# exp(bias) of six heads in PSUM, and the bias of the next unit put in PSUM early, in a streaming log-sum-exp kernel

## The chip, the cores and the metric

The kernel runs on one core of a Trainium2 chip. The metric is the device time of one execution in microseconds (us). A run's profile also gives a span, from the first to the last instruction, which is some 1.8 us shorter.

## The reference, cut to what matters

```python
B, S, D, H = 8, 2048, 2048, 8          # x: B x S x D fp32 (134 MB), bias: H x 256
x_heads = x.reshape(B, S, H, 256).transpose(0, 2, 1, 3) + bias[None, :, None, :]
x_tiled = np.repeat(x_heads, 2, axis=2)
lse = log-sum-exp of x_tiled over its last axis       # B x H x 2S
```

For each row and head, 256 numbers are summed after an exponential. The kernel doesn't subtract the maximum. It has two ways to bring in the bias: add it before the exponential, or multiply by exp(bias) after it.

## The kernel before

x comes in 64 tiles of 128 partitions x 2 rows x 2048 columns (2 MB) into nine SBUF buffers. The work of each tile is shared by heads:

- **Heads of `pe`** (0 and 1, or 0 alone in tiles 50 to 60): TensorE puts the bias in PSUM with a matmul of ones, adds x with a matmul by the identity, and ScalarE takes exp and the sum in one instruction.
- **Heads from `g0`**: GpSimd adds the bias in place, ScalarE takes exp, VectorE sums.
- **The heads between**: ScalarE takes exp of x alone, and VectorE multiplies by exp(bias) and sums.

The last three tiles (61 to 63) go row by row with no GpSimd addition: heads 2 to 7 are all weighed on VectorE by `weigh`, one instruction per row and head, except that GpSimd *folds* head 7 of tile 62's second row and heads 6 and 7 of tile 63's first row: it multiplies them by exp(bias) and halves them by additions to 32 columns, which VectorE reduces.

```python
W0, G0, W1 = Dh, 4 * Dh, 5 * Dh
w_sb = sb.tile([P, D - W1], F32, name="w_sb")        # exp(bias), heads 5 to 7, SBUF
w_ps = pp.tile([P, W1 - W0], F32, name="w_ps")       # exp(bias), heads 1 to 4, 2 PSUM banks
ps = [pp.tile([P, MM], F32, name=f"ps{i}") for i in range(5)]   # biased rows, 5 banks
tpair = pp.tile([P, 2, K, P], F32, name="tpair")     # transpositions, 1 bank
# ... (cut)
def add_bias(m, t, k0, k1):                          # a unit: a tile, or a row of it
    for ka, kb in groups:
        nc.tensor.matmul(p[:, ...], lhsT=ones3, rhs=each_row(b3, ...), start=True, stop=False)
    for (ka, kb), views in zip(groups, got):
        mm = nc.tensor.matmul(..., lhsT=ident, rhs=xt[:, ka:kb, 0:n], start=False, stop=True)
# ... (cut)
def weigh(t, v, h, dst, after):
    w = w_ps[...] if c < W1 else w_sb[...]
    nc.vector.tensor_tensor_reduce(out=v, in0=v, in1=w, op0=ALU.mult, op1=ALU.add, accum_out=dst, ...)
def fold(t, k, h0, h1, sums, after):
    nc.gpsimd.tensor_tensor(out=v, in0=v, in1=w_sb[...], op=ALU.mult)
    # ... halving additions on GpSimd, then a short tensor_reduce on VectorE (cut)
```

Of the kernel before, what the change touches and what calls it, by code (L numbers as in the profile page):

```python
# [9 lines left out]
F32 = mybir.dt.float32  # L10
# [6 lines left out]
NBUF = 9  # L17
# [29 lines left out]
def kernel(  # L47
# [7 lines left out]
    P = nc.NUM_PARTITIONS  # L55
    B, S, D = x.shape
    H, Dh = bias.shape
    assert D == H * Dh and S % (P * K) == 0
    NBLK = S // (P * K)
    T = B * NBLK  # L60
    CPE = 2 * Dh
    MM = 512

    W0, G0, W1 = Dh, 4 * Dh, 5 * Dh

    sb = ctx.enter_context(tc.tile_pool(name="sb", bufs=1))
    pp = ctx.enter_context(
        tc.tile_pool(name="pp", bufs=1, space=bass.MemoryType.PSUM)
    )
# [3 lines left out]
    w_sb = sb.tile([P, D - W1], F32, name="w_sb")  # L73
# [9 lines left out]
    res = sb.tile([H * NBLK, B - 1, P, K, 2], F32, name="res")  # L83
    res_last = sb.tile([P, P, 2], F32, name="res_last")
    xts = [sb.tile([P, K, D], F32, name=f"xt{i}") for i in range(NBUF)]
    w_ps = pp.tile([P, W1 - W0], F32, name="w_ps")
    ps = [pp.tile([P, MM], F32, name=f"ps{i}") for i in range(5)]
    tpair = pp.tile([P, 2, K, P], F32, name="tpair")
    tps = [tpair[:, i] for i in range(2)]

    def modes_of(t):
        return [modes for t0, modes in STAGES if t0 <= t][-1]

    def pieces(t):

        if len(modes_of(t)) == 1:
            return [(0, K, 0, D)]
        cols = [[(0, D)]] * K if t < T - 1 else LAST_COLS
        return [(k, k + 1, c0, c1) for k in range(K) for c0, c1 in cols[k]]
# [13 lines left out]
    def on_x(t, ins, after):  # L113
        known = [u for u in users[t] if u.ins.engine != ins.ins.engine]
        for before in range(t % NBUF, t, NBUF):
            known += users[before]
        for u in known:
            if u not in after:
                tc.declare_no_dep(
                    ins.ins, u.ins, reason="waited for by those it waits for"  # L120
                )
        users[t].append(ins)
        return ins
# [21 lines left out]
    for set_idx, (_name, funcs) in enumerate(get_activation_tables(nc.m.arch).items()):  # L145
        if ACT.Exp in funcs and ACT.Ln in funcs:
            nc.scalar.add_instruction(
                mybir.InstLoadActFuncSet(
                    name=nc.get_next_instruction_name(),
# [22 lines left out]
    def spread(dst, c0, c1):  # L172
        nc.tensor.matmul(  # L173
            dst, lhsT=ones, rhs=brow[:, c0:c1], start=True, stop=True
        )

    for i, c in enumerate(range(G0, D, MM)):
# [1 line left out]
        nc.scalar.activation(  # L179
            out=b_rep[:, c - G0 : c - G0 + MM], in_=ps[i], func=ACT.Copy  # L180
        )
    for c in range(W0, W1, MM):
        w = w_ps[:, c - W0 : c - W0 + MM]
        spread(w, c, c + MM)
        nc.scalar.activation(out=w, in_=w, func=ACT.Exp)  # L185
# [2 lines left out]

    n_ps = [0]

    def add_bias(m, t, k0, k1):


        n = m["pe"] * Dh
        xt = xts[t % NBUF]
        step = MM // n
        groups = [(k, min(k + step, k1)) for k in range(k0, k1, step)]
        got = []
        for ka, kb in groups:
            p = ps[n_ps[0] % len(ps)]  # L200
            n_ps[0] += 1
            nc.tensor.matmul(  # L202
                p[:, 0 : (kb - ka) * n],
                lhsT=ones3,
                rhs=each_row(b3, 0, n, kb - ka),
                start=True,
                stop=False,
            )
            got.append([p[:, k * n : (k + 1) * n] for k in range(kb - ka)])
        rows = []  # L210
        for (ka, kb), views in zip(groups, got):
            p = views[0]
            mm = nc.tensor.matmul(  # L213
                bass.AP(
                    tensor=p.tensor,
                    offset=p.offset,
                    ap=[p.ap[0], [1, (kb - ka) * n]],
                ),
                lhsT=ident,
                rhs=xt[:, ka:kb, 0:n],  # L220
                start=False,
                stop=True,
            )
            on_x(t, mm, [loads[t, k0, 0]])
            rows += [(v, mm) for v in views]
        return rows

    def sum_biased(m, t, k, p, mm, sums):
# [11 lines left out]
    def each_row(src, c, n, k_rows):  # L240

        return bass.AP(
            tensor=src.tensor,
            offset=src.offset + c,
            ap=[src.ap[0], [0, k_rows], [1, n]],
        )

    def g_add(m, t, k0, k1):
        c = m["g0"] * Dh
        v = xts[t % NBUF][:, k0:k1, c:D]  # L250
        add = nc.gpsimd.tensor_tensor(  # L251
            out=v, in0=v, in1=each_row(b_rep, c - G0, D - c, k1 - k0), op=ALU.add
        )
        return on_x(t, add, [loads[t, k0, 0]])

    def exp_inplace(t, v, after):
        return on_x(t, nc.scalar.activation(out=v, in_=v, func=ACT.Exp), [after])  # L257
# [23 lines left out]

    def weigh(t, v, h, dst, after):
        c = h * Dh
        w = w_ps[:, c - W0 : c - W0 + Dh] if c < W1 else w_sb[:, c - W1 : c - W1 + Dh]
        ttr = nc.vector.tensor_tensor_reduce(  # L285
            out=v,
            in0=v,
            in1=w,
            scale=1.0,
            scalar=0.0,  # L290
            op0=ALU.mult,
            op1=ALU.add,
            accum_out=dst,
        )
        last_uses[t].append(on_x(t, ttr, [after]))

    def fold(t, k, h0, h1, sums, after):


        v = xts[t % NBUF][:, k, h0 * Dh : h1 * Dh]  # L300
        done = nc.gpsimd.tensor_tensor(  # L301
            out=v, in0=v, in1=w_sb[:, h0 * Dh - W1 : h1 * Dh - W1], op=ALU.mult
        )
        on_x(t, done, [after])
        v = v.rearrange("p (h j) -> p h j", j=Dh)
        n = Dh
        while n > FOLD:
            n //= 2
            done = nc.gpsimd.tensor_tensor(  # L309
                out=v[:, :, 0:n], in0=v[:, :, 0:n], in1=v[:, :, n : 2 * n], op=ALU.add  # L310
            )
            on_x(t, done, [])

        def add_up():
            red = nc.vector.tensor_reduce(
                out=sums[:, k, h0:h1],
                in_=v[:, :, 0:FOLD],
                op=ALU.add,
                axis=mybir.AxisListType.X,
            )  # L320
            on_x(t, red, [done])

        return add_up
# [40 lines left out]
    def sums_of(t):  # L364

        b, blk = divmod(t, NBLK)
        if b < B - 1:
            return R[b][:, :, :, blk]
        return R_last[:, :, blk, :].rearrange("p h k -> p k h")
# [3 lines left out]
    for_pool = []  # L373
    for_pe = []

    def flush(later_work):
        for f in later_work:
            f()
        later_work.clear()

    for t in range(T):
        xt = xts[t % NBUF]
        sums = sums_of(t)
        for k0, k1, c0, c1 in pieces(t):
            m = modes_of(t)[k0]
            add = None
            if c0 == 0:
                got = add_bias(m, t, k0, k1)
                if m["g0"] < H:
                    add = g_add(m, t, k0, k1)  # L390
            if c0 == 0 and (t < T - 1 or k0 == 0):
                flush(for_pool)
            h0 = max(c0 // Dh, m["pe"])
            h1 = min(c1 // Dh, m["g0"])
            hf = max(h0, min(h1, H - m["fold"]))
            if h0 < h1 and not m["late"]:
                done = exp_inplace(
                    t, xt[:, k0:k1, h0 * Dh : h1 * Dh], loads[t, k0, c0]
                )
                if hf < h1:  # L400
                    for_pool.append(fold(t, k0, hf, h1, sums, done))
            if c0 == 0 and (t < T - 1 or k0 == 0):
                flush(for_pe)
            if not m["late"]:
                for k in range(k0, k1):
                    for h in range(h0, hf):
                        weigh(
                            t,
                            xt[:, k, h * Dh : (h + 1) * Dh],
                            h,  # L410
                            sums[:, k, h : h + 1],
                            done,
                        )

            def pool_part(t=t, m=m, k0=k0, k1=k1, sums=sums, add=add):
                if add:
                    later(m, t, k0, k1, sums, add)
                if k1 == K and t + NBUF < T:
                    load(t + NBUF)

            def pe_part(t=t, m=m, got=got, k0=k0, k1=k1, sums=sums):
                for k in range(k0, k1):
                    sum_biased(m, t, k, *got[k - k0], sums)

            for_pool.append(pool_part)
            if c0 == 0:
                if m["g0"] < H:
                    pe_part()
                else:
                    for_pe.append(pe_part)  # L430

        fb, at = divmod(t - 2, NBLK)
        if fb >= 0 and at == NBLK - 1:
            finish(fb)
            if fb == B - 2:
                store()
    flush(for_pe)
    flush(for_pool)
    finish_last()
# [32 lines left out]
```

## Time and profile before

| | before |
|---|---|
| time, median of the first 3 runs | 329.07 us (328.91 to 329.17) |
| span of the profiled run (its time: 328.65 us) | 326.8 us |
| x read | 134.23 MB, at 427 GB/s from 92 to 295 us |
| busy: VectorE, ScalarE, GpSimd, TensorE | 88%, 85%, 88%, 71% |
| last VectorE sum ends, transposition starts | 323.2, 323.45 us |

Read it from the last row up. The DMA engines are busy until nearly the end, and what remains after the last x has landed is a chain through the engines. Only work on that chain can move the end.

### The profile page before, as it was taken

The page shows a single profiled execution, that of the slowest core. Times are in us where ns is not written, and L with a number is a line of the kernel's source. Part 1 is how long each engine was busy: PE and PEld are TensorE (multiplying, and loading weights), DVE is VectorE, ACT ScalarE, POOL GpSimd, SP SyncE. Part 2 cuts the span into 40 slices and gives each one's busy share as a digit, 9 for nine tenths or more (in the row PEclk, how much of TensorE's full clock was granted, in tenths as well). Part 3 has the DMA queues.
Part 4 walks back from the last instruction along what each step waited for, and adds up shares of the span by engine and source line. Part 5 has one row for each costly group of instructions (what it writes and reads, how often), then busy time and mean ns, then how long its engine had stood idle before and what let it go on. Part 6 is the DMA issues. An engine that isn't in the chain of part 4 may idle for free.

```text
span 326.8 us, 1954 instructions
## 1 busy us (share of the span) xinstructions
PE 231.0 (71%) x389; PEld 67.6 (21%) x389; DVE 287.5 (88%) x318; ACT 277.7 (85%) x573; POOL 288.6 (88%) x88
## 2 busy tenths in 40 slices
PE   5499666667897689667658767767678756665784
PEld 2023211112221212211212212212212101222210
DVE  0019999999999999999998999999998999999995
ACT  3269999699889888989889889899888988799994
POOL 6999899979999999999999999999998999999623
PEclk9999898598568955887698778778965555555577
DMA  8999999999999999999999999999999999999993
GB/s 294 432 429 435 422 429 429 427 425 435 419 435 428 421 437 424 425 433 425 426 434 419 424 437 421 431 431 423 433 428 421 439 423 420 421 420 419 421 384 91
DMA packets 11807, 135.41 MB, mean 414 GB/s; under 512 B 1361, under 2 KB 1489, under 8 KB 2833
## 3 DMA queue, kind: packets, MB, share of 16 engines
q1 hardware_dynamic: 11696, 135.27, 98.3%
q8 instruction: 3, 0.05, 0.1%
q14 instruction: 10, 0.08, 0.1%
q10 hardware_dynamic: 2, 0.01, 0.0%
q0 software_dynamic: 96, 0.00, 0.0%
HBM read 134.23 MB, written 1.05 MB: 414 GB/s over the span
## 4 chain that ended last, share of the span: by engine, by line
DMA 58%; DVE 21%; ACT 8%; POOL 8%; PE 4%; issue 1%; SPq 0%; DVEq 0%
DMA xt<-in_x_dram 55%; DVE R L274 14%; ACT xt L257 7%; POOL xt L251 6%; DVE xt L267 5%; PE ps L213 3%; DMA b<-bparts 2%; DVE xt L285 1%; ACT xt L232 1%; DMA brow<-in_bias_dram 1%; PE ps L202 1%; POOL xt L309 0%; POOL brest L164 0%; POOL brest L166 0%; POOL xt L301 0%
## 5 line engine op out<-in xcount | busy, mean ns | idle before, releaser
L251 POOL TENSOR_TENSOR xt<-xt,b_rep 128x2048 f32<-128x2048 f32 (+1 forms) x66 | 277.4, 4212 | 21.1 <-DMA xt<-in_x_dram 21.0
L213 PE MATMUL ps<-xt,ident 128*128 128x512 f32 (+1 forms) x244 | 177.8, 861 | 75.0 <-DMA xt<-in_x_dram 74.8
L257 ACT ACTIVATE xt<-xt 128x3072 f32<-128x3072 f32 (+3 forms) x91 | 185.6, 2063 | 18.6 <-POOL xt L251 18.2
L274 DVE TENSOR_REDUCE R<-xt 128x12 f32<-128x3072 f32 (+1 forms) x56 | 181.4, 3240 | 2.0 <-ACT xt L257 0.3
L232 ACT ACTIVATE xt<-ps 128x256 f32<-128x256 f32 x234 | 87.0, 396 | 15.9 <-PE ps L213 15.7
L267 DVE TENSOR_TENSOR xt<-xt,w_ps 128x1024 f32<-128x1024 f32 x50 | 60.9, 1218 | 32.8 <-ACT xt L257 32.7
L213 PEld LDWEIGHTS ps<-xt,ident 128*128 128x128 f32 x244 | 55.5, 257 | 153.5 <-DMA xt<-in_x_dram 111.6
L202 PE MATMUL ps<-b,ones 3*128 3x512 bf16 (+1 forms) x122 | 48.3, 463 | 6.1 <-DMA b<-bparts 3.7
L232 ACT ACTIVATION_READ_ACCUMULATOR xt<-ps 128x1 f32 x234 | 51.6, 222 | 0.0
L285 DVE CUSTOM_DVE_ANT_0 xt<-xt,w_ps 128x256 f32<-128x256 f32 x84 | 30.2, 416 | 0.0
L202 PEld LDWEIGHTS <-ones 3*128 3x128 bf16 x122 | 7.9, 97 | 79.7 <-issue 79.7
L274 DVE TENSOR_REDUCE R_last<-xt 128x4 f32<-128x1024 f32 x10 | 12.2, 1217 | 0.0
L301 POOL TENSOR_TENSOR xt<-xt,w_sb 128x256 f32<-128x256 f32 (+1 forms) x2 | 2.1, 1057 | 8.5 <-ACT xt L257 8.5
L330 PE MATMUL tpair<-ident,R 128*64 128x128 f32 x14 | 3.5, 340 | 5.8 <-DVE R L274 5.8
L285 DVE CUSTOM_DVE_ANT_0 xt<-xt,w_sb 128x256 f32<-128x256 f32 x15 | 6.8, 495 | 0.0
L173 PE MATMUL ps<-brow,ones 1*128 1x512 f32 x4 | 3.7, 1089 | 3.4 <-DMA brow<-in_bias_dram 3.4
L340 ACT ACTIVATE res<-tpair 64x512 f32<-64x512 f32 x7 | 4.1, 582 | 2.2 <-PE tpair L330 2.2
L285 DVE DVE_READ_ACCUMULATOR2_ANT R_last<- 128x1 f32 x63 | 5.2, 82 | 0.0
L179 ACT ACTIVATE b_rep<-ps 128x512 f32<-128x512 f32 x2 | 1.2, 597 | 4.6 <-PE ps L173 4.6
L173 PE MATMUL w_ps<-brow,ones 1*128 1x512 f32 x4 | 4.0, 1096 | 0.7 <-ACT w_ps L185 0.7
L330 PEld LDWEIGHTS tpair<-ident,R 128*64 128x64 f32 x14 | 1.7, 140 | 12.0 <-DVE R L274 9.7
L185 ACT ACTIVATE w_ps<-w_ps 128x512 f32<-128x512 f32 x2 | 1.2, 582 | 3.3 <-PE w_ps L173 3.3
(24 smaller groups left out, 18.3 us busy)
## 6 DMA issues: line engine op xcount, KB each, us to landing
xt<-in_x_dram SPq DMA_DIRECT2D x56, 2048.0 KB, 31.9
xt<-in_x_dram SPq DMA_DIRECT2D x14, 1024.0 KB, 21.0
xt<-in_x_dram SPq DMA_DIRECT2D x5, 256.0 KB, 11.3
out_dram<-res SPq DMA_DIRECT2D x1, 896.0 KB, 7.9
xt<-in_x_dram SPq DMA_DIRECT2D x2, 384.0 KB, 16.5
out_dram<-res_last SPq DMA_DIRECT2D x1, 128.0 KB, 1.7
b<-bparts POOLq DMA_DIRECT2D x3, 1.0 KB, 5.6
brow<-in_bias_dram ACTq DMA_DIRECT2D x1, 8.0 KB
```

What stands on the lines that cost most here:

```text
L173: nc.tensor.matmul(dst, lhsT=ones, rhs=brow[:, c0:c1], start=True, stop=True)
L202: nc.tensor.matmul(p[:, 0 : (kb - ka) * n], lhsT=ones3, rhs=each_row(b3, 0, n, kb - ka), start=True, stop=False,)
L213: mm = nc.tensor.matmul(bass.AP(tensor=p.tensor, offset=p.offset, ap=[p.ap[0], [1, (kb - ka) * n]],), lhsT=ident, rhs=xt[:, ka:kb, 0:n], s ...
L232: act = nc.scalar.activation(out=xts[t % NBUF][:, k, c : c + Dh], in_=p[:, c : c + Dh], func=ACT.Exp, accum_out=sums[:, k, h : h + 1],)
L251: add = nc.gpsimd.tensor_tensor(out=v, in0=v, in1=each_row(b_rep, c - G0, D - c, k1 - k0), op=ALU.add)
L257: return on_x(t, nc.scalar.activation(out=v, in_=v, func=ACT.Exp), [after])
L267: mul = nc.vector.tensor_tensor(out=f, in0=f, in1=each_row(w_ps, h0 * Dh - W0, n, k1 - k0), op=ALU.mult,)
L274: red = nc.vector.tensor_reduce(out=sums[:, k0:k1, h0:H], in_=v.rearrange("p k (h j) -> p k h j", j=Dh), op=ALU.add, axis=mybir.AxisListTy ...
L285: ttr = nc.vector.tensor_tensor_reduce(out=v, in0=v, in1=w, scale=1.0, scalar=0.0, op0=ALU.mult, op1=ALU.add, accum_out=dst,)
L301: done = nc.gpsimd.tensor_tensor(out=v, in0=v, in1=w_sb[:, h0 * Dh - W1 : h1 * Dh - W1], op=ALU.mult)
L330: nc.tensor.transpose(out=tp[0:nr, k], in_=R[b][:, k].rearrange("p h n -> p (h n)"), identity=ident,)
L340: nc.scalar.activation(out=res[:, b], in_=tv, func=ACT.Ln)
```

## The change

The intent is twofold. Heads 5 and 6 join those whose exp(bias) lies in PSUM; w_ps grows from two banks to three, and the biased rows lose a bank. And TensorE is to have the bias of the next unit in PSUM already when its x lands.

```diff
-    W0, G0, W1 = Dh, 4 * Dh, 5 * Dh
+    W0, G0, W1, W2 = Dh, 4 * Dh, 6 * Dh, 7 * Dh
...
-    w_ps = pp.tile([P, W1 - W0], F32, name="w_ps")
-    ps = [pp.tile([P, MM], F32, name=f"ps{i}") for i in range(5)]
+    w_ps = pp.tile([P, W2 - W0], F32, name="w_ps")
+    ps = [pp.tile([P, MM], F32, name=f"ps{i}") for i in range(4)]
...
-    for c in range(W0, W1, MM):
+    for c in range(W0, W2, MM):
...
-    def add_bias(m, t, k0, k1):
+    def put_bias(m, k0, k1):        # the bias matmuls of a unit
...
+    def add_x(m, t, k0, got):       # its x matmuls
...
-        w = w_ps[...] if c < W1 else w_sb[...]
+        w = w_ps[...] if c < W2 else w_sb[...]
...
+    bias_there = put_bias(*next_units.pop(0))
...
-                got = add_bias(m, t, k0, k1)
+                got = add_x(m, t, k0, bias_there)
+                if next_units:
+                    bias_there = put_bias(*next_units.pop(0))
```

More of the change, by code (lines that the diff above doesn't have):

```diff
@@ L189 @@
     n_ps = [0]
-    def add_bias(m, t, k0, k1):
+    def put_bias(m, k0, k1):
         n = m["pe"] * Dh
-        xt = xts[t % NBUF]
         step = MM // n
-        groups = [(k, min(k + step, k1)) for k in range(k0, k1, step)]
         got = []
-        for ka, kb in groups:
-            p = ps[n_ps[0] % len(ps)]
+        for ka in range(k0, k1, step):
+            kb = min(ka + step, k1)
+            p = ps[n_ps[0] % len(ps)][:, 0 : (kb - ka) * n]
             n_ps[0] += 1
             nc.tensor.matmul(
-                p[:, 0 : (kb - ka) * n],
+                p,
                 lhsT=ones3,
@@ L208, in add_bias @@
             )
-            got.append([p[:, k * n : (k + 1) * n] for k in range(kb - ka)])
+            got.append((ka, kb, p))
+        return got
+    def add_x(m, t, k0, got):
+        n = m["pe"] * Dh
         rows = []
-        for (ka, kb), views in zip(groups, got):
-            p = views[0]
+        for ka, kb, p in got:
             mm = nc.tensor.matmul(
-                bass.AP(
-                    tensor=p.tensor,
-                    offset=p.offset,
-                    ap=[p.ap[0], [1, (kb - ka) * n]],
-                ),
+                p,
                 lhsT=ident,
-                rhs=xt[:, ka:kb, 0:n],
+                rhs=xts[t % NBUF][:, ka:kb, 0:n],
                 start=False,
@@ L224, in add_bias @@
             on_x(t, mm, [loads[t, k0, 0]])
-            rows += [(v, mm) for v in views]
+            rows += [(p[:, k * n : (k + 1) * n], mm) for k in range(kb - ka)]
         return rows
@@ L283, in weigh @@
         c = h * Dh
-        w = w_ps[:, c - W0 : c - W0 + Dh] if c < W1 else w_sb[:, c - W1 : c - W1 + Dh]
+        w = w_ps[:, c - W0 : c - W0 + Dh] if c < W2 else w_sb[:, c - W1 : c - W1 + Dh]
         ttr = nc.vector.tensor_tensor_reduce(
@@ L374 @@
     for_pe = []
+    next_units = [
+        (modes_of(t)[k0], k0, k1)
+        for t in range(T)
+        for k0, k1, c0, _ in pieces(t)
+        if c0 == 0
+    ]
+    bias_there = put_bias(*next_units.pop(0))
     def flush(later_work):
```

## The prediction

> **What bounds the kernel now.** I read the time of every engine first, then the slices of the span, then the chain that ended last, and then the tail instruction by instruction, because each of these views sends the reader on to the next. From the profile page of the kernel before, the slices:
>
> ```profile
> DVE  0019999999999999999998999999998999999995
> ACT  3269999699889888989889889899888988799994
> POOL 6999899979999999999999999999998999999623
> DMA  8999999999999999999999999999999999999993
> q1 hardware_dynamic: 11696, 135.27, 98.3%
> HBM read 134.23 MB, written 1.05 MB: 414 GB/s over the span
> ```
>
> The DMA row is at nine tenths from the second slice to the last but one, and the queue of the x loads takes 98.3% of what the 16 engines have. Table of stretches: 427 GB/s from 92 to 295 us and 423 from 295 to 310. At 427 GB/s the 134.23 MB take 314 us of a span of 326.8. So the body of the kernel is a stream of x; VectorE (88%), ScalarE (85%) and GpSimd (88%) follow just behind. Something that shortens only their work or TensorE's in the body cannot bring the end forward. The remaining 12 us or so lie after the last data, and there an engine's work counts. The chain of waits of the last 12 us (start us, duration us, what):
>
> ```profile
> 294.92 19.81 DMA xt<-in_x_dram
> ...
> 314.75 1.49 ACT xt L257
> ...
> 316.31 0.86 POOL xt L301
> ...
> 318.58 0.19 DVE R_last L315
> 318.76 1.31 DVE xt L285
> ...
> 320.09 0.33 DVE xt L285
> ...
> 322.83 0.34 DVE xt L285
> ...
> 323.45 0.32 PE tpair L351
> ```
>
> The end is set by VectorE: after the reduction at 318.58, eleven weighted sums (exp(x) times exp(bias), summed over a head, L285) run without a gap; ten of them step by 0.34 us, the first takes 1.31 us of the chain. Then come a short reduction, one transposition, one logarithm and the store, 326.8 - 323.45 = 3.35 us that the change does not touch. The timeline shows who that first one is and what is beside it (start us, duration us, engine, line, operation):
>
> ```profile
> 317.90 0.53 DVE L285 CUSTOM_DVE_ANT_0 xt<-xt,w_sb 128x256 f32<-128x256 f32 x1
> 318.53 1.27 POOL L301 TENSOR_TENSOR xt<-xt,w_sb 128x512 f32<-128x512 f32 x1
> 318.68 1.40 DVE L285 CUSTOM_DVE_ANT_0 xt<-xt,w_sb 128x256 f32<-128x256 f32 x1
> 320.01 0.41 DVE L285 CUSTOM_DVE_ANT_0 xt<-xt,w_ps 128x256 f32<-128x256 f32 x1
> ```
>
> The slow one takes its weight from SBUF (w_sb), starts 0.15 us after a GpSimd multiply of two SBUF operands, and ends at 320.08, 0.28 us after GpSimd does (319.80). Its neighbour with the weight in PSUM takes 0.41 us. By tile: 15 instructions with w_sb take 414/422/1398 ns (shortest/median/longest), 84 with w_ps 408/416/422. PSUM itself is no faster; it only escapes what GpSimd does.
>
> **What the Trainium skill says.** "SBUF — State Buffer", section "Who interferes with whom": VectorE and GpSimd share a pair of ports under an exclusive lock; a VectorE instruction with two SBUF inputs contends with a GpSimd one that reads SBUF, whichever comes first blocks the other for a whole instruction, and a VectorE instruction with at most one SBUF input, outside the two-port modes, does not contend. The trace agrees: 1.40 us against 0.42, and never over 0.422 us in 84 cases with w_ps. "PSUM — Partial Sum Buffer", "Specifications (TRN2)": 8 banks of 512 fp32 values per partition. So w_ps goes from 2 banks to 3, the biased rows (ps) from 5 to 4, and the transpositions keep 1: PSUM is full in both. The same page, "Engine vs sequencer instructions": matmuls start and complete in program order. That decides what the second half of the change can do; the trace's TensorE rows indeed alternate in program order.
>
> **The change, part by part.**
>
> *Bias of the next unit early.* In the program text the bias matmuls move from just ahead of their x matmuls to just behind the x matmuls of the unit before. I compared TensorE's two instruction streams: both are bias 0, x 0, bias 1, x 1, and so on. Nothing lay between x of one unit and the bias of the next except the transpositions of a finished batch, 14 in all at 340 ns (3.5 us); those now stand behind the bias. And before the change the bias already ran ahead of its data: the waits table has TensorE waiting 74.8 us for x in 58 cases, with the bias 3.7 us for its first load and 2.3 us for ScalarE, and nothing else. At 140.66 us the two bias matmuls run, 0.60 us, and the x matmuls follow at 141.94 when their data land. Only 7 pairs of transpositions change place, at most 7 x 0.6 us, all where TensorE waits for x afterwards. Worth to the end: 0.
>
> *Four banks instead of five.* In the body a unit takes two banks. With five, the second bias matmul waits for the first half of the sums of two units back; with four, for the second half, two ScalarE instructions or about 0.36 x 2 = 0.7 us later. The trace shows such waits twice, at 33.13 us (0.76) and 37.24 us (1.51), while ScalarE catches up with the nine tiles loaded at the start. They may become three or four, each up to 0.7 us longer. At that time VectorE has 4 to 5 tiles of backlog and waits for nothing until 91 us, and the loads are queued 31.9 us from issue to landing. In the tail a unit takes one bank: the last bias (319.32) needs the bank of four units back, whose sums ended at 314.4. Worth: 0.
>
> *A third piece of w_ps.* One more fp32 matmul (1.06 us) and one more exp (0.58 us), and 0.25 us less exp for w_sb. Before, the second exp ended at 12.25 us and TensorE then waited until 15.36 us for the bias rows. The third piece: matmul 12.3 to 14.4, exp to 15.0, w_sb until 15.6. ScalarE's first sum is at 18.40. It fits by about 1 us. Worth: 0.
>
> *Heads 5 and 6 weighed from PSUM.* Of the 15 instructions with w_sb only the four of head 7 remain w_sb. (The unit with head 7 folded on GpSimd and the last tile's first row use none on VectorE.) Eight of the eleven that move run at 0.42 either way: nothing. The two at 317.52 (0.46) and 317.90 (0.53) save 0.04 and 0.11, but the reduction at 318.58 that follows waits for GpSimd's fold, which ended at 318.55: hidden. The one at 318.68 goes from 1.40 to 0.41 us and is on the chain: 1.31 - 0.34 = 0.97 us off VectorE.
>
> How much of 0.97 us reaches the end? VectorE then runs behind ScalarE's five exponentials (317.61 to 320.74; 842 ns for the two of 768 columns, 622 for three of 512, overlapping by about 0.1). The second one ends at 317.61 + 0.73 + 0.84 = 319.2, and VectorE would be ready at 319.02: it loses 0.2. Nine sums are then left at 0.34 (three of the first row, six of the second, whose exponentials end at 319.7, 320.2 and 320.74, each in time): 319.25 + 9 x 0.34 = 322.3, plus the reduction 0.21 = 322.5, against 323.3 before. VectorE saves 0.8. But the transposition also needs ScalarE's last sum of the biased heads, which ends at 322.65, released by TensorE's last x matmul (319.85 to 321.78). So the transposition starts at about 322.65 + 0.14 = 322.8 instead of 323.45. The sum is 0.65 us.
>
> **Rivals.**
>
> *A. Full gain of 1 us.* This needs ScalarE's last sum to come earlier as well. TensorE's chain in the tail is load at 314.75, x 2.0, bias 0.5, x 2.0, bias 0.5, x 1.9, at a granted clock of 0.66. If a higher clock is granted there, it shortens by some tenths. The change doesn't cause that. Time: 328.0.
>
> *B. The wait on ScalarE takes the place of the removed one altogether*, or the fold does: GpSimd's last instruction ends at 319.88 + 1.73 = 321.61, and the last reduction waits for it. That is 0.7 us before VectorE gets there, and GpSimd's multiply, no longer met by a VectorE instruction on SBUF, can only end earlier. So the fold is no bound; but if the tail's matmuls get a clock nearer 0.5, the gain shrinks to 0.2 or so. Time: 328.9.
>
> *C. Four banks stall TensorE and through it the sums, the release of buffers and the loads.* This would need TensorE to fall so far behind that a load is issued late; the DMA row would show a dip. Against it: 16 us between the first release (28 us) and the time the stream of nine tiles (4.85 us each) would run dry at 44, and TensorE's idle 75 us. A case of 1 to 3 us is conceivable: 330 to 332. I give it 3%.
>
> *D. TensorE's lead brings the x matmuls forward.* It would show as less waiting of ScalarE for TensorE (15.7 us now). Since the order is the same, I expect none.
>
> **Range and chances.** The median of before is 329.07 us, three runs within 0.26. 329.07 - 0.65 = 328.4. The stream of 134 MB adds its own scatter between builds: 0.1% of its rate is 0.3 us. With A and B at the edges, the range is 327.7 to 329.2. Two per cent would be 6.6 us, more than half of all that lies after the stream, so faster by over 2% has 1%, slower 2%, and within 2% 97%.
>
> **What would show it.** Right: the VectorE weighted sum beside GpSimd's multiply of 512 columns takes 0.41 to 0.42 us; no w_ps instruction exceeds 0.43; the chain before the last transposition passes through ScalarE's sum (L232) or is level with VectorE's; the transposition starts about 0.6 us earlier relative to the last load's landing; DMA stays at 420 GB/s and more. Wrong: a DMA slice below nine tenths in the body, waits of TensorE's bias matmul for ScalarE over some 10 us in sum, a w_ps instruction as slow as 1 us, or a time that moves by over 2 us. The weakest term is the stream itself: a change of its rate by 0.3% would hide all of the gain.

## The result, and the profile after

In the first comparison the changed kernel took 328.07 us (median of 6 runs, 328.03 to 328.42) against 329.0 (6 runs, 328.9 to 329.18): ratio 0.9973, 95% interval 0.996 to 0.9986. Two later sets, below, gave 0.9988 and 0.999, with intervals that reach just above 1: at most some 0.3% faster, never slower by the medians, and in the later sets not told apart from no change.

The slices of the span from the page of the changed kernel, with the load queue:

```profile
DVE  0029999999999999989998999989998999999994
ACT  3279999798889888799889889899888988799995
POOL 7999899979999999999998999999998999999713
DMA  8999999999999999999999999999999999999993
q1 hardware_dynamic: 11696, 135.27, 98.5%
```

The DMA row is the same digit by digit, and the rate from 92 to 295 us is 427 GB/s as before. The body hasn't moved; the span is 326.5 instead of 326.8. The chain that ended last in the changed kernel, its last pieces (start us, duration us, what):

```profile
309.90 10.19 DMA xt<-in_x_dram
...
320.12 0.63 ACT xt L257
...
321.38 1.47 ACT xt L232 x8
322.85 0.04 issue
322.89 0.49 PE tpair L351
```

VectorE is gone from these pieces. The chain is now: x lands, ScalarE's last two exponentials, its four sums of the biased heads, transposition. And the timeline at the place of the slow sum:

```profile
318.53 0.19 DVE L315 TENSOR_REDUCE R_last<-xt 128x1 f32<-128x32 f32 x1 [0.17 <-POOL xt L309]
318.63 1.27 POOL L301 TENSOR_TENSOR xt<-xt,w_sb 128x512 f32<-128x512 f32 x1
318.64 0.41 DVE L285 CUSTOM_DVE_ANT_0 xt<-xt,w_ps 128x256 f32<-128x256 f32 x1
...
319.32 0.42 DVE L285 CUSTOM_DVE_ANT_0 xt<-xt,w_ps 128x256 f32<-128x256 f32 x1 [0.26 <-ACT xt L257]
...
320.12 1.27 ACT L257 ACTIVATE xt<-xt 128x512 f32<-128x512 f32 x2 [0.31 <-DMA xt<-in_x_dram]
```

GpSimd's multiply and VectorE's sum start within 0.01 us of each other and neither is lengthened: 1.27 and 0.41 us. In the kernel before the sum took 1.40. By tile, the shortest, median and longest of all weighted sums of the changed kernel, first those with weights in SBUF, then in PSUM:

```profile
L285 DVE CUSTOM_DVE_ANT_0 xt<-xt,w_sb x4: 420/422/422, 312.1 to 322.1; 128x256 f32<-128x256 f32 x4
L285 DVE CUSTOM_DVE_ANT_0 xt<-xt,w_ps x95: 410/418/422, 262.7 to 321.7; 128x256 f32<-128x256 f32 x95
```

No sum is slow any more.

### The profile page after: what moved, and what is told of

It is laid out like the page before. It is cut to its first block, busy times and chain, and to the rows that moved or that the text cites. A ratio compares the mean times of both kernels' runs of the same rounds, so it can differ in the third digit from the quotient of the medians.

```text
span 326.5 us, 1959 instructions
## 1 busy us (share of the span) xinstructions
PE 230.7 (71%) x391; PEld 67.5 (21%) x391; DVE 286.4 (88%) x318; ACT 278.5 (85%) x574; POOL 288.4 (88%) x88
## 4 chain that ended last, share of the span: by engine, by line
DMA 69%; DVE 10%; POOL 7%; ACT 7%; PE 6%; issue 0%; SPq 0%
DMA xt<-in_x_dram 67%; DVE R L274 7%; POOL xt L251 6%; ACT xt L257 5%; PE ps L217 4%; DVE xt L267 2%; DMA b<-bparts 2%; ACT xt L232 2%; PE ps L202 1%; DMA brow<-in_bias_dram 0%; POOL brest L165 0%; POOL brest L167 0%; POOL b L170 0%; PE tpair L330 0%; POOL bparts L164 0%
## 5 line engine op out<-in xcount | busy, mean ns | idle before, releaser
L217 PE MATMUL ps<-xt,ident 128*128 128x512 f32 (+1 forms) x244 | 175.7, 852 | 78.8 <-DMA xt<-in_x_dram 78.5
L232 ACT ACTIVATE xt<-ps 128x256 f32<-128x256 f32 x234 | 86.8, 394 | 11.2 <-PE ps L217 11.1
L202 PE MATMUL ps<-b,ones 3*128 3x512 bf16 (+1 forms) x122 | 47.5, 457 | 2.8 <-ACT xt L232 1.6
L285 DVE CUSTOM_DVE_ANT_0 xt<-xt,w_ps 128x256 f32<-128x256 f32 x95 | 34.0, 417 | 0.3 <-ACT xt L257 0.3
L174 PE MATMUL w_ps<-brow,ones 1*128 1x512 f32 x6 | 6.0, 1109 | 1.3 <-ACT w_ps L186 1.3
L285 DVE DVE_READ_ACCUMULATOR2_ANT R<- 128x1 f32 x36 | 3.0, 85 | 0.0
```

Of the source, the lines that this page charges most:

```text
L174: nc.tensor.matmul(dst, lhsT=ones, rhs=brow[:, c0:c1], start=True, stop=True)
L202: nc.tensor.matmul(p, lhsT=ones3, rhs=each_row(b3, 0, n, kb - ka), start=True, stop=False,)
L217: mm = nc.tensor.matmul(p, lhsT=ident, rhs=xts[t % NBUF][:, ka:kb, 0:n], start=False, stop=True,)
L232: act = nc.scalar.activation(out=xts[t % NBUF][:, k, c : c + Dh], in_=p[:, c : c + Dh], func=ACT.Exp, accum_out=sums[:, k, h : h + 1],)
L285: ttr = nc.vector.tensor_tensor_reduce(out=v, in0=v, in1=w, scale=1.0, scalar=0.0, op0=ALU.mult, op1=ALU.add, accum_out=dst,)
```

## The experiments

The theory to test: one VectorE instruction (head 5 of the last tile's first row) used to wait for GpSimd, and this is the whole gain. The rivals: the early bias gives it; the bank less costs something; the other ten moved sums matter. Twelve runs were made, in three sets of four: ten new kernels, and the changed kernel twice more; all gave right results. The edits are shortened, and some are shown against the changed kernel ("after, but").

**First set: the parts of the change one by one.** The kernel before took 328.89 us here (9 runs, 328.77 to 329.38).

*weights_only*: three banks of weights and four of biased rows, the bias matmuls where they were.

```diff
 (after, but)
-                got = add_x(m, t, k0, bias_there); bias_there = put_bias(...)
+                got = add_bias(m, t, k0, k1)
```

> Six heads of exp(bias) in PSUM and four banks for the biased rows, but the bias matmuls where they were before the change. Theory (one weighted sum of VectorE in the tail no longer waits for GpSimd): the whole gain of the change is here, 0.6 to 1.0 us less than the kernel before, and the sum beside GpSimd's 512-column multiply takes 0.42 us. Rival (the bias put in PSUM early gives the gain): no gain, within 0.2 us of before.

Measured: 328.25 us (328.11 to 328.86), ratio 0.9982 (0.9969 to 0.9994), and no w_ps sum over 0.422 us. The gain is here, as expected. (In its only trace VectorE started 0.04 us before GpSimd; that matters below.)

*order_only*: the early bias with four heads of weights and five banks.

```diff
 (after, but)
-    W0, G0, W1, W2 = Dh, 4 * Dh, 6 * Dh, 7 * Dh
+    W0, G0, W1, W2 = Dh, 4 * Dh, 5 * Dh, 5 * Dh
-    ... for i in range(4)]
+    ... for i in range(5)]
```

> The bias of the next unit early, but four heads in PSUM and five banks as before the change. Theory: within 0.2 us of the kernel before, because TensorE's order is the same but for 14 transpositions; the slow sum still takes about 1.4 us. Rival (bias early gives the gain): 0.6 to 1.0 us faster.

Measured: 328.76 us (328.25 to 329.1), ratio 0.9993 (0.998 to 1.0005), so the same within what the runs resolve. From its timeline:

```profile
318.65 1.27 POOL L301 TENSOR_TENSOR xt<-xt,w_sb 128x512 f32<-128x512 f32 x1
318.73 1.47 DVE L285 CUSTOM_DVE_ANT_0 xt<-xt,w_sb 128x256 f32<-128x256 f32 x1
```

The slow sum is still there, as expected. But the runs spread over 0.85 us, and one was as fast as the changed kernel.

*banks_only*: the kernel before with `range(4)` for `range(5)` banks, nothing else.

> The kernel before with four banks for the biased rows instead of five, nothing else. Theory: within 0.2 us of before; TensorE's bias matmuls wait for ScalarE somewhat more often (2 to 4 times, 2 to 4 us in sum), all in the first 45 us. Rival (a bank less costs time which the change had to win back): 0.3 us or more slower.

Measured: 328.74 us (328.27 to 329.16), ratio 0.9995 (0.9981 to 1.0008). The bias matmuls waited for ScalarE four times, 2.3 us in all; before it was two times and also 2.3 us. The bank less costs nothing that the runs resolve. Its profile, of a run of 328.39 us, held the surprise:

```profile
318.77 0.42 DVE L285 CUSTOM_DVE_ANT_0 xt<-xt,w_sb 128x256 f32<-128x256 f32 x1
318.81 1.51 POOL L301 TENSOR_TENSOR xt<-xt,w_sb 128x512 f32<-128x512 f32 x1 [0.19 <-ACT xt L257]
```

The same instruction, weights in SBUF, beside the same multiply, takes 0.42 us. VectorE started 0.04 us ahead of GpSimd, and it is GpSimd that was lengthened, from 1.27 to 1.51 us. That costs little: GpSimd's additions end later, and one VectorE sum of the second row, with its weight in SBUF, took 0.53 us beside them. The slow sum of the kernel before isn't a fixed cost: it depends on which engine starts first, and the margin is some hundredths of a microsecond (0.15 in before, 0.04 the other way here).

*one_from_psum*: the kernel before with the third piece of weights and four banks, but only the one instruction uses it.

```diff
+        in_ps = W2 if (t, k) == (T - 1, 0) else W1
-        w = w_ps[...] if c < W1 else w_sb[...]
+        w = w_ps[...] if c < in_ps else w_sb[...]
```

> The kernel before with the third piece of weights made in PSUM and four banks, but only one instruction uses it: head 5 of the last tile's first row. The other 14 keep their weights in SBUF. Theory: this one instruction is the whole gain, so 0.5 to 1.0 us faster than before, as fast as the changed kernel within 0.2 us. Rival (several of the eleven moved sums count): half of the gain or less, under 0.4 us.

Measured: 328.29 us (328.03 to 328.78), ratio 0.998 (0.9968 to 0.9993): by the runs, the gain of weights_only from one instruction in place of eleven. Its timeline:

```profile
319.17 0.42 DVE L286 CUSTOM_DVE_ANT_0 xt<-xt,w_ps 128x256 f32<-128x256 f32 x1
319.22 1.28 POOL L302 TENSOR_TENSOR xt<-xt,w_sb 128x512 f32<-128x512 f32 x1 [0.18 <-ACT xt L257]
```

VectorE was first here too, and banks_only shows that it then takes 0.42 us with its weight in SBUF as well. So this trace can't tell the PSUM operand from the earlier start. In all six traces with this sum's weight in PSUM (three of the changed kernel, weights_only, this one, tail) VectorE starts between 0.05 us before GpSimd and 0.01 us after it. That the operand alone is enough in the tail rests on these five runs, whose times overlap with those of banks_only; that it escapes the block as such is shown by mixed_from_sbuf, below.

**Second set: is it needed, and is it the meeting with GpSimd?** Before: 328.61 us (9 runs, 328.27 to 329.05). It was run on another chip. The kernel before itself is faster here and spreads wider.

*after_again*: the changed kernel.

> The changed kernel once more, on the same chip as the next runs. 0.6 to 1.0 us faster than before, all runs close together (within 0.4 us), because no instruction of the tail depends any more on whether VectorE or GpSimd starts first.

Measured: 328.29 us (328.04 to 328.48), ratio 0.9988 (0.9974 to 1.0001). The spread is as expected; the gain isn't. It is 0.3 us by the medians. Against the first comparison, before is 0.4 us faster here and the changed kernel 0.2 us slower.

*one_back*: the changed kernel with that one instruction taking its weight from SBUF again.

```diff
+        in_ps = W1 if (t, k) == (T - 1, 0) else W2     # with W1 = 5 * Dh
```

> The changed kernel with one instruction put back: head 5 of the last tile's first row takes its weight from SBUF again; the other ten keep PSUM, and the bias is early. Theory: the gain is gone or nearly (within 0.3 us of before) in runs where GpSimd's multiply starts first, and kept where VectorE starts first, as the traces of two earlier runs (1.47 us and 0.42 us for the same instruction) suggest; so a median between, and runs spread over 0.6 us or more. Rival (ten other moved sums or the early bias): 0.6 us or more faster in every run.

Measured: 328.23 us (328.14 to 328.55), ratio 0.999 (0.9977 to 1.0002), and every run within 0.1 us of the range of the changed kernel. The theory's expectation of a wide spread failed (0.4 us, not 0.6), and so did the rival's of 0.6 us or more in every run. The timeline says why:

```profile
318.67 0.18 DVE L316 TENSOR_REDUCE R_last<-xt 128x1 f32<-128x32 f32 x1 [0.16 <-POOL xt L310]
318.77 0.42 DVE L286 CUSTOM_DVE_ANT_0 xt<-xt,w_sb 128x256 f32<-128x256 f32 x1
318.82 1.51 POOL L302 TENSOR_TENSOR xt<-xt,w_sb 128x512 f32<-128x512 f32 x1 [0.18 <-ACT xt L257]
```

VectorE was first again, by 0.05 us. This has a cause. The sum follows a short reduction, which waits for GpSimd's fold of tile 62. In the kernel before, VectorE's sums of heads 5 and 6 of that tile run beside this fold with both operands in SBUF, and each slows the other: they take 0.46 and 0.53 us instead of 0.42, the fold's three additions 1.31 us instead of 1.19 in the changed kernel. Counted from the start of ScalarE's last exponential of tile 62, which is the landing of its x, the reduction begins:

| traces | reduction after that start, us |
|---|---|
| those two sums with weights in SBUF (before, order_only, banks_only, head5_later, pool_late, dve_late, one_from_psum) | 3.73 to 3.83 |
| in PSUM (the three of the changed kernel, weights_only, one_back, tail) | 3.60 to 3.65 |

For example, 318.58 - 314.75 = 3.83 before and 318.67 - 315.07 = 3.60 in one_back. VectorE thus comes 0.1 to 0.2 us earlier to the meeting, while GpSimd's multiply waits for ScalarE's exponential. So, in this trace, the ten other sums give the gain too, in this other way, and the changed kernel may owe its gain to it as well. In banks_only and one_from_psum it was GpSimd that came later: its multiply began 3.88 and 3.89 us after that start, in before and order_only 3.78, because ScalarE reached the exponential that it waits for 0.1 us later.

*head5_later*: the kernel before, head 5 of that row taken after heads 2 to 4.

```diff
-                        weigh(...)
+                        if (t, k, h) == (T - 1, 0, 5): put_off.append(args)
+                        else: weigh(*args)
+                if (t, k0, c0) == (T - 1, 0, 512): weigh(*put_off.pop())
```

> The kernel before, with all weights of heads 5 to 7 in SBUF, but in the last tile's first row VectorE takes head 5 after heads 2 to 4 instead of before, so that it no longer meets GpSimd's 512-column multiply. Theory (a block by GpSimd, not PSUM as such): 0.2 to 0.6 us faster than before; head 5 takes 0.42 to 0.8 us because a smaller GpSimd addition may be beside it. Rival (PSUM operands matter by themselves): no gain, within 0.15 us.

Measured: 328.6 us (328.54 to 329.27), ratio 1.0003 (0.999 to 1.0015): no gain, and the expectation failed.

```profile
318.63 1.27 POOL L301 TENSOR_TENSOR xt<-xt,w_sb 128x512 f32<-128x512 f32 x1
319.98 1.72 POOL L309 TENSOR_TENSOR xt<-xt 128x256 f32<-128x256 f32 x3
320.35 0.64 DVE L285 CUSTOM_DVE_ANT_0 xt<-xt,w_sb 128x256 f32<-128x256 f32 x1
```

The sum did escape the long multiply, and took 0.64 us beside the smaller additions. But heads 2 to 4 can't start before their exponential, the second of five (0.84 us long), so VectorE stood idle for some 0.5 us that head 5 had filled. A block was exchanged for a wait. I had left that wait out.

*mixed_from_sbuf*: a dose of the suspected cost. In the changed kernel the 66 sums of tiles 50 to 60 take their weights from an SBUF copy, beside GpSimd's long additions.

```diff
+    nc.scalar.activation(out=w_low, in_=w_ps[:, 0 : 3 * Dh], func=ACT.Copy)
+        if t < 61:
+            w = w_low[:, c - W0 : c - W0 + Dh]
```

> A dose of the suspected cost: the changed kernel, but in tiles 50 to 60, where GpSimd adds the bias nearly without a pause, the 66 weighted sums of heads 1 to 3 take their weights from an SBUF copy. Theory: many of them wait for the end of a GpSimd instruction of 2.3 or 4.5 us; their mean is 0.8 to 1.5 us instead of 0.42, some take over 2 us, and the kernel is 5 to 25 us slower as VectorE has no idle time there. Rival (no block, the one slow sum was an accident): mean 0.42 us, time unchanged.

Measured: 364.35 us (2 runs), ratio 1.1086 (1.1065 to 1.1106). The group and two lines of the timeline:

```profile
L289 DVE CUSTOM_DVE_ANT_0 xt<-xt,w_low 128x256 f32<-128x256 f32 x66 | 60.7, 974 | 0.0
```

```profile
265.70 4.63 POOL L253 TENSOR_TENSOR xt<-xt,b_rep 128x2048 f32<-128x2048 f32 x1 [0.37 <-DMA xt<-in_x_dram]
265.89 4.73 DVE L289 CUSTOM_DVE_ANT_0 xt<-xt,w_low 128x256 f32<-128x256 f32 x1
```

A sum of 0.42 us becomes one of 4.73 us: it starts 0.19 us after GpSimd's addition and ends 0.29 us after it. In all, 14 of the 66 sums took 2.5 to 4.74 us; none of the others took over 0.425. In the changed kernel the same 66 sums, with PSUM weights beside the same additions, never took over 0.422. The mean rose to 974 ns as expected, and the kernel lost more than expected: 66 x (0.974 - 0.416) = 36.8 us of VectorE, and 364.35 - 328.29 = 36.1 us of time against the changed kernel of the same set, so nothing is absorbed. The load stream can't hide it, since the buffers come free late: the DMA share falls to 0.71 between 259 and 348 us. The block by GpSimd is real and large where GpSimd's instructions are long.

**Third set: decide the start on purpose, and try to beat both.** Before: 328.47 us (9 runs, 328.23 to 328.99). It was run on another chip.

*pool_late*: the kernel before with a useless GpSimd instruction ahead of the multiply.

```diff
+        if t == T - 1:
+            nc.gpsimd.memset(pause, 0.0)
         done = nc.gpsimd.tensor_tensor(out=v, in0=v, in1=w_sb[...], op=ALU.mult)
```

> The kernel before with one useless instruction more: GpSimd writes zeros to a 128x256 scratch tile just ahead of its multiply in the last tile, so that VectorE's head 5 starts first every time. Weights in SBUF and five banks as before. Theory (the gain is who starts first): as fast as the changed kernel, 328.0 to 328.5 us in every run, head 5 takes 0.42 us in the profile. Rivals (PSUM operands, early bias): no gain, or slower by the added 0.3 us.

```profile
318.71 0.30 POOL L303 MEMSET pause<- 128x256 f32 x1
...
318.90 0.41 DVE L286 CUSTOM_DVE_ANT_0 xt<-xt,w_sb 128x256 f32<-128x256 f32 x1
318.98 1.47 POOL L304 TENSOR_TENSOR xt<-xt,w_sb 128x512 f32<-128x512 f32 x1
```

Measured: 328.2 us (328.0 to 328.46), ratio 0.9988 (0.9975 to 1.0). By the runs and the trace as expected: a useless instruction makes the old kernel as fast as the changed one, with no weight moved and no bank taken.

*dve_late*: the same on VectorE, ahead of head 5.

```diff
+                        if (t, k, h) == (T - 1, 0, 5):
+                            nc.vector.memset(pause, 0.0)
                         weigh(
```

> The counterpart: the kernel before with VectorE writing zeros to a 128x256 scratch tile just ahead of head 5, so that GpSimd's multiply starts first every time. Theory: every run on the slow side, 328.7 us or more, 0.5 to 0.9 us slower than the run with GpSimd late; head 5 ends 0.2 to 0.4 us after GpSimd's multiply, whatever its start. Rival (who starts first doesn't matter): both runs differ by less than 0.2 us.

```profile
318.75 1.27 POOL L302 TENSOR_TENSOR xt<-xt,w_sb 128x512 f32<-128x512 f32 x1
318.84 0.27 DVE L409 MEMSET pause<- 128x256 f32 x1
319.03 1.27 DVE L286 CUSTOM_DVE_ANT_0 xt<-xt,w_sb 128x256 f32<-128x256 f32 x1
```

Measured: 328.48 us (328.32 to 329.0), ratio 0.9995 (0.9982 to 1.0009). In the trace (a run of 329.0 us) it is as expected: GpSimd first, the sum ends 0.28 us after the multiply, the transposition at 323.68 us against 323.16 in pool_late. The times follow only in part. The medians differ by 0.28 us, the intervals overlap, and three of the five runs (328.32, 328.41, 328.48) lie below the 328.7 us that the theory allowed, two of them as fast as the changed kernel. No trace of those runs was kept; why they were fast is open.

*after_third*: the changed kernel once more.

> The changed kernel on the same chip as its neighbours: within 0.2 us of the run with GpSimd late, 0.5 to 0.9 us faster than the run with VectorE late.

Measured: 328.36 us (328.12 to 328.51), ratio 0.999 (0.9978 to 1.0003). It is within 0.2 us of pool_late as expected, but only 0.12 us by the medians ahead of dve_late.

*tail*: an attempt at a better kernel than both, in two small edits to the changed one.

```diff
-            if fb == B - 2:
-                store()
+                if t == T - 1:                         # after tile 62's fold
+                    nc.gpsimd.tensor_copy(one, one)    # one element of res
+                    store()
+            if (t, k0, c0) == (T - 1, 1, 1024):
+                for_pe.pop(0)()                        # first row's sums earlier on ScalarE
```

> An attempt to beat both: the changed kernel, with ScalarE's sums of the last tile's first row ahead of its last two exponentials (where it waits 0.3 us for x), and the 896 KB store of the first seven batches held back by a one-element GpSimd copy until about 318.6 us, so that it doesn't compete with the last loads. Expected: the last x pieces land up to 0.5 us earlier; the bound goes to VectorE's row of sums, so 0.2 to 0.4 us faster than the changed kernel. It is slower if the store, late, gets in the way of the final store.

Measured: 328.58 us (328.19 to 328.77), ratio 0.9997 (0.9984 to 1.0009), so faster than neither. Its chain passes through VectorE's last reduction again:

```profile
322.61 0.14 DVE R_last L315
322.76 0.14 issue
322.89 0.46 PE tpair L351
```

The transposition starts at 322.89 us, just as in the changed kernel: the sums came earlier, but VectorE's row of sums ends no sooner. The last two pieces of x landed as late as in the changed kernel (10.2 and 8.3 us after issue), though the store was held back, so the store isn't what makes them late. What made most of its runs slower isn't known; the store, now issued at 318.70 us with 6.3 us to landing, reaches to about 325 us, past the issue of the final store at 323.79, but no run had that alone.

**The tail by itself.** The time of a run mixes the load stream with the tail. In the thirteen traces of these kernels (mixed_from_sbuf left out) ScalarE's last exponential of tile 62, which starts when its x has landed, starts anywhere from 314.75 us (before) to 315.33 us (one_from_psum). The time of each profiled run minus that start leaves the tail:

| traces | tail, us |
|---|---|
| sum behind GpSimd (before, order_only, dve_late) | 13.90, 13.89, 14.11 |
| head5_later | 13.66 |
| weight in SBUF, VectorE first (banks_only, pool_late, one_back) | 13.46, 13.45, 13.16 |
| weight in PSUM (changed kernel three times, weights_only, one_from_psum, tail) | 13.37, 13.37, 13.36, 13.36, 13.45, 13.24 |

So the tail is 0.4 to 0.7 us shorter wherever the sum isn't slow and not moved, with its weight in PSUM or in SBUF, and no trace contradicts this. The trace of head5_later has a tail 0.24 us shorter than before's, which its five times don't show. The landing scatters by as much as the gain.

## Why the prediction was right or wrong

The time lies in the range, and the mechanism that the prediction names is in the traces. By its own steps:

- **Bias of the next unit early, worth 0.** Not contradicted: order_only 0.9993, interval 0.998 to 1.0005, which would still allow 0.7 us, but its trace has the tail of before (13.89 and 13.90 us). TensorE waited 71.1 to 78.5 us for x in the three traces of the changed kernel, 74.8 before. (The prediction's 3.5 us for 14 transpositions of 340 ns is their busy time, overlaps counted once.)
- **Four banks, worth 0.** Not contradicted (banks_only 0.9995). The predicted rise of the waits was too high: 2.3 us in four places in banks_only, 1.6 to 2.9 us in three to six places in the traces of the changed kernel.
- **A third piece of w_ps, fits by about 1 us.** Right at the start: after its last matmul TensorE still waited 1.0 us for the bias rows. At the end something came along with it that the prediction didn't see, told below the transposition. (Its "one more fp32 matmul (1.06 us)" is two of them, 2.07 us in the trace, as its own times 12.3 to 14.4 have it.)
- **Head 5 from PSUM, 1.40 to 0.41 us.** Right in the profile. The runs of one_from_psum go with it, but one_back reaches 0.42 us with SBUF too, so whether the operand or the earlier start did it in the changed kernel isn't separated.
- **Eleven weighted sums without a gap, ten of them in steps of 0.34 us.** Miscounted: the chain has ten, and nine step. The later sum, "9 x 0.34", uses the right number.
- **"The remaining 12 us or so lie after the last data."** They lie after the landing of tile 62. Pieces of tile 63 were still landing: in the changed kernel ScalarE waited for one until 320.12 us, 6.4 us before the end of the span.
- **VectorE's last reduction ends at 322.5.** It ended at 322.40 + 0.22 = 322.62, in a run whose x of tile 62 landed 0.13 us later.
- **The transposition starts at 322.8, held by ScalarE's last sum, "released by TensorE's last x matmul".** The time is right (322.89) and ScalarE's sum is what held it, but its releaser is wrong: TensorE's last x matmul was done at 318.16 + 1.13 = 319.29. ScalarE was late because its fourth exponential waited until 320.12 for x.
- **What delays that x, which the prediction lacks.** In the six traces with the third piece in PSUM where this can be seen (three of the changed kernel, weights_only, one_back, one_from_psum) ScalarE stands idle there, for 0.27 to 0.31 us in four and 0.1 us in weights_only and one_from_psum; in the six without (before, order_only, banks_only, head5_later, pool_late, dve_late) it doesn't. The record narrows the reason: in all seven traces with the third piece the last two loads of x take about 10.2 and 8.3 us from issue to landing, in the six without about 9.5 and 7.7, so the early bias and the bank less are not the reason. And between 318 and 320.4 us those seven show one 8 KB packet of the queue q14, which the profile calls "instruction", and the six show none. No run moved this packet alone, so that it delays the loads isn't shown. The cost is small: VectorE's last reduction would have let the transposition start at about 322.76, 0.13 us earlier (an estimate from 322.62 and the 0.14 us between the two before).
- **"Hidden": the 0.04 and 0.11 us of the two sums beside the fold.** This step was incomplete. They gain nothing directly, but without them the fold ends earlier and VectorE comes first to the meeting (one_back). Nor do the sums of the last row always "run at 0.42 either way": with SBUF weights, where GpSimd's last additions came later, they took 0.53 us (banks_only), 0.56 and 0.53 (pool_late) and 0.55 (one_from_psum).
- **The sum of 0.65 us.** It took the slow sum of one trace for a constant. For that trace the size is right: the transposition starts 8.70 us after tile 62's landing before (323.45 - 314.75) and 8.01 after (322.89 - 314.88), 0.69 us less. Of this, 0.53 us reaches the end (13.90 - 13.37), because the transposition itself took 0.49 us in place of 0.32; that isn't the change's doing, since banks_only, pool_late and dve_late have 0.46 too. The first comparison gave 0.93 us by the medians, the later ones 0.32 and 0.11; the mean of the three ratios is 0.9984, which is 0.5 us. Over those sets after went from 328.07 to 328.36 and before from 329.0 to 328.47, so both moved. The scatter of the landing, 0.58 us among the traces, is enough to hide or to double a gain of 0.5 us; how much of the 0.1 to 0.9 us it made can't be told, as runs without a trace have no landing. That the kernel before itself sometimes has VectorE first may be, since a variant that differs by one PSUM bank had it (banks_only), but its only trace shows GpSimd first. The fast runs of dve_late (328.32, 328.41) would need a landing at 314.2 to 314.3 us with the tail of its trace, earlier than in any trace, so they stay open.

Of the rivals, B's form came closest (the chain moved to ScalarE), with another cause. C didn't occur. D's sign did appear, ScalarE's wait for TensorE fell from 15.7 to 11.1 us (15.0 and 11.7 in the other two traces of the changed kernel); but with the early bias alone it was 16.9 (order_only), so the early bias isn't the cause.

## What to carry to other kernels

Where VectorE and GpSimd both read two SBUF operands at the same time, look at both engines' starts before you call the longer instruction a cost: a few hundredths of a microsecond may decide who pays, and a variant or two in the profile shows it. Compare tails counted from the last comparable landing, not only whole times: here the landing scattered by as much as the gain. A PSUM operand on VectorE takes the question away; a moved GpSimd instruction can, too, and where GpSimd's instructions last 4.5 us the difference was 36 us. In a kernel bound by its load stream, count a change only by what it moves after the last landing, and look for the next wait behind the one removed: here it left 0.69 of the 0.97 us at the transposition.

## What the Trainium skill lacked or had wrong

- "SBUF — State Buffer", "Who interferes with whom": its rule held in the cases looked at here, in both directions: a sum of 0.42 us took 1.27 to 1.47 us beside the 512-column multiply and 4.73 beside an addition of 4.63 us; GpSimd's multiply rose from 1.27 to 1.47 and 1.51 us when VectorE was first. It names tensor_tensor for two SBUF inputs; the multiply-and-sum of this kernel (tensor_tensor_reduce) isn't among the operations listed by name, and behaves as its general rule says.
- The same section says that the loser is blocked for the whole instruction; it doesn't give what remains after the release. Here the sum ended 0.28 us (before, dve_late) and 0.29 us (mixed_from_sbuf) after GpSimd, less than its own 0.41 us.
- The same section says that the order of issue decides who blocks. It doesn't warn that builds of one kernel can fall on either side: starts 0.15 us apart one way in before, 0.04 us the other way in banks_only.
